# Two-layer transformer block on one core: modulation vectors turned into columns through memory, in portions of 512 columns

## The chip, the cores and the metric

The kernel runs on one core of a Trainium2 chip. The metric is the device time of one execution in microseconds (us); the time of before is the median of three runs. A profile is one execution recorded by the hardware profiler. The engines are PE (TensorE, matmuls) with its weight loads (PEld), DVE (VectorE), ACT (ScalarE), POOL (GpSimd) and SP (SyncE, which issues most of the DMAs). A letter q behind an engine's name means its queue of issued instructions.

## The reference

Two layers, each with a mixer (a gated recurrence, neighbourhood attention and sliding-window attention side by side) and a mixture of 16 experts, over 256 tokens `x` and 256 context tokens `ctx`, all in fp32. Each layer's mixing and normalisation is modulated by six vectors of 1024 numbers, once for `x` and once for `ctx`; these are what the change touches:

```python
D_MODEL = 1024; SEQ = 256; CTX_LEN = 256; DEPTH = 2
def ada_mod(cond, w, b):
    m = (jax.nn.silu(cond) @ w + b)[..., None, :]
    return jnp.split(m, 6, axis=-1)
...
for l in range(DEPTH):
    sh1, sc1, g1, sh2, sc2, g2 = ada_mod(c, w_ada[l], b_ada[l])
    csh1, csc1, cg1, csh2, csc2, cg2 = ada_mod(c_ctx, w_ada[l], b_ada[l])
    h = x * (1.0 + sc1) + sh1;  hc = ctx * (1.0 + csc1) + csh1
    y, yc = mixer(h, hc, ...)
    x = layer_norm(alpha * x + g1 * y, ...);  h2 = x * (1.0 + sc2) + sh2
    f = moe(h2, ...);  x = layer_norm(alpha * x + g2 * f, ...)
    # the same for ctx, except in the last layer
```

`w_ada` has 1024 x 6144 fp32 numbers in each layer, 24 MB, of which each is read once.

## The kernel before

The kernel keeps tokens as columns (feature on the partition), so a modulation vector is wanted as columns: `mod[l]` is a tile of 128 partitions x 6 vectors x 8 blocks x 2 (one for `x`, one for `ctx`). The first two vectors of layer 0 are made at the start, in four short calls of `ada` with their own tiles (`xtp`), and are not touched by the change but for the name of the array that they are loaded from. The other ten vectors of the two layers are made under way, in 20 *portions*: a portion is half a vector, 512 of its 1024 columns, with 2 MB of weights. Portions 0 to 13 run in layer 0's mixer (eight for the other four vectors of layer 0, six for the first three of layer 1), portions 14 to 19 in layer 1's.

A portion is one call of `fill()`, which pops the next from a list and calls `ada`. The calls are woven by hand between projections (`proj`, line 432), attention heads and the recurrence (`weave`, with the counts `FILLS`), and a scheduler then orders each engine's instructions with the program's order as priority. Nothing in the mixer waits for a portion soon: `vectors(0)`, called after portion 7, forms the vectors that layer 0's end uses, sends them to memory (`vd<-md`, line 687, issued by ACT), from which SP loads them back as broadcast rows (line 690).

In a portion, `ada` does this. Two loads of 1 MB go through POOL's queue (line 404) into the two slots of a ring; each waits until PE has read what the slot held, which is the portion before. Then 16 matmuls, each with two columns of the condition (padded to 32) as the stationary operand and 256 columns of weights moving, in four column groups of the array: block `kb` goes to group `kb % 4`, so that four partial sums stand at partitions 0, 32, 64 and 96 of a PSUM bank. Eight use the first slot, eight the second. The trace shows two records for each fp32 matmul, so 32 a portion. ACT copies the bank to SBUF (`vt`, line 414), PE transposes the four 128 x 128 pieces (`adaT`, line 417, a PSUM bank of its own), DVE adds the four partial sums (line 419) and the bias (line 424, two instructions).

The tile `vt` has two buffers and is also used by other copies of ACT. POOL has little else to do in the mixers: the additions of line 1023 in the recurrence, which wait for DVE, and a few fills with a constant.

Of the kernel before, what the change touches and what calls it, by code (L numbers as in the profile page):

```python
# [16 lines left out]
OP = mybir.AluOpType  # L17
AX = mybir.AxisListType

P = 128  # L20
D = 1024
KB = 8
NX = 256
NT = 512
DEPTH = 2
# [38 lines left out]
PIECE = 8 * K  # L64
# [69 lines left out]
def _layout(inp):  # L134
    g = {k: np.asarray(v) for k, v in inp.items()}
    o = {}
# [3 lines left out]
    w = g["w_ada"].reshape(DEPTH, P, KB, 6, P, 4, 2)  # L140
    o["w_ada"] = w.transpose(0, 3, 5, 1, 2, 6, 4).reshape(DEPTH, 24, P, PIECE)
    o["b_ada"] = g["b_ada"].reshape(DEPTH, 6, P, KB).transpose(2, 0, 1, 3).reshape(P, DEPTH * 6 * KB)
# [5 lines left out]
    w = g["w_out"][:, rows, :].reshape(DEPTH, 4, 2, P, D)  # L148
# [42 lines left out]
class _Builder:  # L191
# [117 lines left out]
    def setup(self):  # L309
# [8 lines left out]
        def aload(q):  # L318
            for s in (1, 0):
                self.aw[s, q] = self.g(slots.pop(0), PIECE)  # L320
                nc.sync.dma_start(self.aw[s, q], ap["w_ada"][0, 4 * s + q])

# [72 lines left out]

    def ada(self, l, parts, w=None):
        nc = self.nc
        names = ("xtp", "xtp") if w else ("ada", "adaT")
        if w is None:
            w = []  # L400
            for s, q in parts:
                t = self.g(self.aring[self.na % len(self.aring)], PIECE)
                self.na += 1
                self.late(nc.gpsimd.dma_start(t, self.ap["w_ada"][l, 4 * s + q]))  # L404
                w.append(t)
        pb = self.bank(names[0])
        n = 256 * len(parts)
# [6 lines left out]
        nc.scalar.copy(ev, pb[:, :n])  # L414
        pt = self.bank(names[1])
        for k in range(n // P):
# [107 lines left out]
    def fill(self, n=1):  # L524
        for _ in range(n):
            if self.adas:
                a = self.adas.pop(0)
                self.ada(*a)
                if a[1][-1] == (5, 3):
                    self.vectors(a[0])  # L530

    def mixer(self, l):
# [20 lines left out]
        if l == 0:  # L553
            chunk = lambda l, s: [(l, ((s, q), (s, q + 1))) for q in (0, 2)]
            todo = sum([chunk(0, s) for s in (2, 4, 3, 5)] + [chunk(1, s) for s in (1, 0, 2, 4, 3, 5)], [])
            self.todo = [todo[:8 + EARLY], todo[8 + EARLY:]]
# [70 lines left out]
        self.ering = self.E  # L627
        self.fill(len(self.adas) - n[3])
        if not last:
            self.xres(0)  # L630
# [1551 lines left out]
```

## Time and profile before

| | |
|---|---|
| runs of before | 1181.65, 1181.06, 1179.41 us |
| median | 1181.06 us |
| the profiled execution | 1181.6 us |
| its span in the trace | 1179.7 us |
| mean granted clock of PE | 0.951 |
| layer 0: start, mixer, experts | 0 to 62, 62 to 345, 345 to 680 us |
| layer 1: start, mixer, experts | 680 to 740, 740 to 890, 890 to 1180 us |

The stages are cut by eye at round times. The span runs from the first to the last record of the trace; the execution's own time is 1.9 us longer. The chain is the work that ended last, followed back from the last instruction to what released each step.

### The profile page before, as it was taken

How to read it: one execution, taken by the hardware profiler on the slowest of the kernel's cores; microseconds unless marked ns; L12 is line 12 of the kernel's file. 1: busy time of each engine (PE TensorE's matmuls, PEld its weight loads, DVE VectorE, ACT ScalarE, POOL GpSimd, SP SyncE). 2: the span in 40 equal slices, each digit the busy share in tenths (PEclk: the TensorE clock that was granted, in tenths of full speed). 3: DMA queues.
4: the chain of work that ended last, by engine and by line, in shares of the span. 5: the costliest groups of instructions: out<-in, count | busy, mean ns of one | idle time of the engine just before them, and what ended most of it. 6: DMA issues, size and time to landing. Idle time of an engine off the chain costs nothing.

```text
span 1179.7 us, 18296 instructions
## 1 busy us (share of the span) xinstructions
PE 1069.7 (91%) x6813; PEld 692.8 (59%) x6813; DVE 742.9 (63%) x1703; ACT 533.2 (45%) x875; POOL 129.0 (11%) x137
## 2 busy tenths in 40 slices
PE   5999999999995999999999778999999599999992
PEld 3766776665684777677543378667657344444430
DVE  3456788767689999788623685678786923212125
ACT  2363433446543678588633544543555412211122
POOL 0000011100001134344310000110100000000000
PEclk9999999999995999999999989999999599999995
DMA  9756666644375899799999931744549299999991
GB/s 374 272 214 256 246 249 228 239 160 143 108 285 196 298 362 359 277 351 394 371 406 417 406 111 72 253 155 163 180 153 355 83 410 422 422 421 422 422 384 40
DMA packets 55042, 326.87 MB, mean 277 GB/s; under 512 B 9435, under 2 KB 9691, under 8 KB 19616
## 3 DMA queue, kind: packets, MB, share of 16 engines
q1 hardware_dynamic: 43920, 275.34, 60.5%
q0 software_dynamic: 9152, 50.10, 11.4%
q8 instruction: 56, 0.92, 0.3%
q10 hardware_dynamic: 1872, 0.16, 0.1%
q14 instruction: 42, 0.34, 0.1%
HBM read 316.27 MB, written 13.09 MB: 279 GB/s over the span
## 4 chain that ended last, share of the span: by engine, by line
PE 73%; DVE 14%; ACT 4%; DMA 4%; issue 3%; POOL 1%; SPq 0%; DVEq 0%; ACTq 0%; POOLq 0%
PE proj L432 12%; PE gu L185 9%; PE gu L1647 7%; PE dn L185 4%; PE op L727 4%; PE dn L1647 4%; PE gu L1638 4%; PE first L432 3%; PE ada L411 2%; DMA G<-in_w_ada_dram 2%; PE pt L1140 2%; PE dn L1638 2%; PE hgt L185 2%; PE S L1117 2%; PE py L1147 1%
## 5 line engine op out<-in xcount | busy, mean ns | idle before, releaser
L294 ACT CAST S<-G 128x1024 fp32r<-128x1024 f32 (+2 forms) x83 | 79.3, 958 | 82.0 <-PE proj L432 52.8
L294 ACT CAST T<-G 128x1024 fp32r<-128x1024 f32 (+2 forms) x79 | 78.1, 994 | 84.4 <-PE proj L432 56.1
L304 DVE TENSOR_TENSOR S<-G,S 128x1024 fp32r<-128x1024 f32 (+2 forms) x75 | 85.8, 1147 | 43.7 <-ACT S L294 41.8
L185 PE MATMUL gu<-G,C 128*64 128x512 f32 (+2 forms) x464 | 109.0, 618 | 0.7 <-ACT C L1620 0.7
L304 DVE TENSOR_TENSOR T<-G,T 128x1024 fp32r<-128x1024 f32 (+2 forms) x69 | 82.4, 1198 | 40.5 <-ACT T L294 40.1
L432 PE MATMUL proj<-A,T 128*128 128x512 f32 (+1 forms) x336 | 97.3, 363 | 1.5 <-ACT T L294 1.0
L432 PE MATMUL proj<-A,S 128*128 128x256 f32 (+1 forms) x336 | 89.9, 347 | 1.3 <-DVE S L304 0.9
L1957 DVE SCALAR_TENSOR_TENSOR S<-dn,slot,S 128x512 fp32r<-128x512 f32 x17 | 12.8, 751 | 113.1 <-ACT S L1956 113.0
L432 PEld LDWEIGHTS proj<-A,T 128*128 128x128 f32 x336 | 59.7, 189 | 16.7 <-issue 4.6
L185 PEld LDWEIGHTS gu<-G,C 128*64 128x64 f32 (+2 forms) x464 | 32.7, 135 | 57.7 <-issue 54.0
L432 PEld LDWEIGHTS proj<-A,S 128*128 128x128 f32 x336 | 59.6, 194 | 11.5 <-issue 3.1
L1956 ACT ACTIVATE S<-dn,slot 128x512 fp32r<-128x512 f32 x17 | 11.7, 687 | 89.5 <-PE dn L185 89.5
L1647 PE MATMUL gu<-C,A 128*128 128x512 f32 (+3 forms) x180 | 48.9, 403 | 2.1 <-DVE C L304 2.1
L1647 PE MATMUL gu<-T,A 128*128 128x512 f32 (+3 forms) x174 | 47.6, 404 | 3.3 <-POOL T L302 2.2
L404 POOL DMA_DIRECT2D G<-in_w_ada_dram x40 | 22.1, 552 | 258.6 <-PE ada L411 179.3
L185 PE MATMUL dn<-G,A 128*64 128x512 f32 (+2 forms) x224 | 48.9, 635 | 0.4 <-ACT A L1620 0.4
L1590 POOL DMA_INDIRECT G<-h2d,idx x16 | 22.4, 1397 | 219.7 <-DVE oh L1574 140.7
L294 ACT CAST C<-G 128x1024 fp32r<-128x1024 f32 x38 | 39.8, 1047 | 12.5 <-PE gu L1647 7.2
L1129 ACT ACTIVATE G<-G,nm 128x512 f32<-128x512 f32 x48 | 34.4, 719 | 21.2 <-DVE nm L1127 10.8
L1638 PE MATMUL gu<-G,C 128*64 128x512 f32 x192 | 43.0, 595 | 0.0
L989 DVE TENSOR_TENSOR G<-G 128x256 f32<-128x256 f32 x112 | 42.6, 418 | 0.5
L411 PE MATMUL ada<-G,sT 128*32 128x256 f32 x640 | 40.3, 383 | 1.6 <-DMA G<-in_w_ada_dram 1.6
(483 smaller groups left out, 2392.9 us busy)
## 6 DMA issues: line engine op xcount, KB each, us to landing
G<-in_w_gate_dram SPq DMA_DIRECT2D x62, 1024.0 KB, 8.6
G<-in_w_up_dram SPq DMA_DIRECT2D x60, 1024.0 KB, 9.4
G<-in_w_down_dram SPq DMA_DIRECT2D x60, 1024.0 KB, 12.1
G<-in_w_ada_dram POOLq DMA_DIRECT2D x40, 1024.0 KB, 6.7
G<-in_w_in_dram SPq DMA_DIRECT2D x22, 1024.0 KB, 7.5
G<-in_w_out_dram SPq DMA_DIRECT2D x12, 1024.0 KB, 6.3
G<-in_w_ada_dram SPq DMA_DIRECT2D x8, 1024.0 KB, 16.2
G<-vd SPq DMA_DIRECT2D x12, 512.0 KB, 4.5
```

The costliest lines, as they stand in the source:

```text
L185: return self._then(self.b.nc.tensor.matmul(*a, **k))
L294: self.lasts = [self.nc.scalar.copy(hi, raw)]
L304: self.lasts.append(sub(lo, raw, v))
L411: nc.tensor.matmul(pb[g:g + 32, i * 256:(i + 1) * 256], self.sT[:, kb, :], w[i][:, kb * 256:(kb + 1) * 256], start=kb < 4, stop=kb >= 4, t ...
L432: self.nc.tensor.matmul(pb[:, t], a[:, c], m, start=first and n == 0 and i == 0, stop=last and n == len(kbs) - 1 and i == 2)
L727: nc.tensor.matmul(pbs[tb][h], a, w[j][h], start=n == 0 and i == 0, stop=n == KB - 1 and i == 2)
L989: mul = lambda o, v: tt(o, o, v.to_broadcast([P, n, c]), op=OP.mult)
L1117: nc.tensor.matmul(pb, qT[r, qb * P:(qb + 1) * P], kT[r, :], start=True, stop=True)
L1129: nc.scalar.activation(Pt, Pt, AF.Exp, scale=-1.0, bias=m, accum_out=ls[:, i:i + 1])
L1140: nc.tensor.transpose(pt[:, k * P:(k + 1) * P], Ps[i][:, k * P:(k + 1) * P], self.ident)
L1638: self.pe.matmul(pb[t], h[0][:, g + i], w[o // PIECE][:, o % PIECE:o % PIECE + 512], start=g == 0, stop=g + m == nk, tile_position=(0, i * ...
L1647: nc.tensor.matmul(pbs[j][:cap], h[a][:, k], ws[b][:, c], start=k == 0 and q == 0, stop=k == nk - 1 and q == 2)
```

## The change

`ada` stays as it was for the four calls at the start. A portion is now done in three steps. `send` loads, multiplies and writes; `back` reads; `total` adds. The weights are laid out otherwise on the host, so that a slot holds four blocks `kb` of all 512 columns: a portion is 8 matmuls of 512 columns, the first four from the first slot and the last four from the second. After ACT's copy there are no transposes: POOL issues four DMAs, each of two partitions x 512 numbers (the two rows of a partial sum, 4 KB), to a tile of 8 x 512 in memory. `back` is one DMA on SP's queue that reads the 8 rows so that each of the 128 partitions gets four consecutive numbers of each row: 1024 runs of 16 bytes. `total` adds the four partial sums and the bias with two DVE instructions. `fill` issues the read of a portion one portion later, and its sum two or three later; at the end of a layer's list all sums are made, and `drain` does what is left at the end of layer 1's mixer. So `vectors(0)` comes at the call of portion 10 and no longer at that of portion 7.

```diff
--- before.py
+++ after.py
@@ -138,7 +138,9 @@
     o["xT"] = o["xc"].reshape(NT, P, KB).transpose(1, 2, 0).reshape(P, KB * NT)
     o["cc"] = np.stack([g["c"][0], g["c_ctx"]], axis=-1).reshape(P, KB * 2)
     w = g["w_ada"].reshape(DEPTH, P, KB, 6, P, 4, 2)
-    o["w_ada"] = w.transpose(0, 3, 5, 1, 2, 6, 4).reshape(DEPTH, 24, P, PIECE)
+    o["w_ada0"] = w[0, :, :, :2].transpose(2, 4, 0, 1, 5, 3).reshape(8, P, PIECE)
+    w = g["w_ada"].reshape(DEPTH, P, 2, 4, 6, P, 2, 4)
+    o["w_ada"] = w.transpose(0, 4, 6, 2, 1, 3, 5, 7).reshape(DEPTH, 24, P, PIECE)
     o["b_ada"] = g["b_ada"].reshape(DEPTH, 6, P, KB).transpose(2, 0, 1, 3).reshape(P, DEPTH * 6 * KB)
     w = np.stack([g["w_in"][l][:, _columns(l)] for l in range(DEPTH)]).reshape(DEPTH, P, KB, 11, 2, P)
     o["w_in"] = w.transpose(0, 3, 1, 4, 2, 5).reshape(DEPTH, 11, P, PIECE)
@@ -318,7 +320,7 @@
         def aload(q):
             for s in (1, 0):
                 self.aw[s, q] = self.g(slots.pop(0), PIECE)
-                nc.sync.dma_start(self.aw[s, q], ap["w_ada"][0, 4 * s + q])
+                nc.sync.dma_start(self.aw[s, q], ap["w_ada0"][4 * s + q])
 
         self.first = []
         for q in range(4):
@@ -393,17 +395,45 @@
         nc.vector.tensor_scalar_max(self.lb, self.lb, LB_MIN)
         nc.vector.tensor_scalar(self.lb1m, self.lb, -1.0, 1.0, op0=OP.mult, op1=OP.add)
 
-    def ada(self, l, parts, w=None):
+    def send(self, l, s, h):
         nc = self.nc
-        names = ("xtp", "xtp") if w else ("ada", "adaT")
-        if w is None:
-            w = []
-            for s, q in parts:
-                t = self.g(self.aring[self.na % len(self.aring)], PIECE)
-                self.na += 1
-                self.late(nc.gpsimd.dma_start(t, self.ap["w_ada"][l, 4 * s + q]))
-                w.append(t)
-        pb = self.bank(names[0])
+        w = []
+        for j in range(2):
+            t = self.g(self.aring[self.na % len(self.aring)], PIECE)
+            self.na += 1
+            self.late(nc.gpsimd.dma_start(t, self.ap["w_ada"][l, 4 * s + 2 * h + j]))
+            w.append(t)
+        pb = self.bank("ada")
+        for kb in range(KB):
+            g = 32 * (kb % 4)
+            nc.tensor.matmul(pb[g:g + 32], self.sT[:, kb, :], w[kb // 4][:, kb % 4 * 512:(kb % 4 + 1) * 512],
+                             start=kb < 4, stop=kb >= 4, tile_position=(0, g))
+        ev = self.st("vt", 512)
+        nc.scalar.copy(ev, pb)
+        r = self.dram([8, 512], f"ada{l}{s}{h}")
+        for g in range(4):
+            nc.gpsimd.dma_start(r[2 * g:2 * g + 2, :], ev[32 * g:32 * g + 2])
+        self.sent.append((l, s, h, r))
+
+    def back(self):
+        l, s, h, r = self.sent.pop(0)
+        a = self.st("adab", 32)
+        self.nc.sync.dma_start(a.rearrange("p (r n) -> p r n", n=4), r[:, :].rearrange("r (p n) -> p r n", n=4))
+        self.backs.append((l, s, h, a))
+
+    def total(self):
+        l, s, h, a = self.backs.pop(0)
+        red = self.st("adar", 8).rearrange("p (n s) -> p n s", s=2)
+        self.nc.vector.tensor_reduce(red, a.rearrange("p (g s n) -> p n s g", g=4, s=2), axis=AX.X, op=OP.add)
+        o = (l * 6 + s) * KB + 4 * h
+        b = self.s["b_ada"][:, o:o + 4]
+        self.nc.vector.tensor_tensor(self.mod[l][:, s, 4 * h:4 * h + 4], red, b[:, :, None].to_broadcast([P, 4, 2]), op=OP.add)
+        if (s, h) == (5, 1):
+            self.vectors(l)
+
+    def ada(self, l, parts, w):
+        nc = self.nc
+        pb = self.bank("xtp")
         n = 256 * len(parts)
         for i in range(len(parts)):
             for kb in range(KB):
@@ -412,7 +442,7 @@
                                  start=kb < 4, stop=kb >= 4, tile_position=(0, g))
         ev = self.st("vt", 512)[:, :n]
         nc.scalar.copy(ev, pb[:, :n])
-        pt = self.bank(names[1])
+        pt = self.bank("xtp")
         for k in range(n // P):
             nc.tensor.transpose(pt[:, k * P:(k + 1) * P], ev[:, k * P:(k + 1) * P], self.ident)
         red = self.st("adar", 8).rearrange("p (i k s) -> p i k s", s=2, k=2)[:, :len(parts)]
@@ -524,10 +554,17 @@
     def fill(self, n=1):
         for _ in range(n):
             if self.adas:
-                a = self.adas.pop(0)
-                self.ada(*a)
-                if a[1][-1] == (5, 3):
-                    self.vectors(a[0])
+                self.send(*self.adas.pop(0))
+                while len(self.backs) > 1 - (not self.adas):
+                    self.total()
+                if len(self.sent) > 1:
+                    self.back()
+
+    def drain(self):
+        while self.sent:
+            self.back()
+        while self.backs:
+            self.total()
 
     def mixer(self, l):
         self.tokens_in()
@@ -551,7 +588,8 @@
         self.have = set()
         self.npp = self.npt = 0
         if l == 0:
-            chunk = lambda l, s: [(l, ((s, q), (s, q + 1))) for q in (0, 2)]
+            chunk = lambda l, s: [(l, s, h) for h in range(2)]
+            self.sent, self.backs = [], []
             todo = sum([chunk(0, s) for s in (2, 4, 3, 5)] + [chunk(1, s) for s in (1, 0, 2, 4, 3, 5)], [])
             self.todo = [todo[:8 + EARLY], todo[8 + EARLY:]]
         self.adas = self.todo[l]
@@ -626,6 +664,8 @@
         vecs = self.vecs(l)
         self.ering = self.E
         self.fill(len(self.adas) - n[3])
+        if last:
+            self.drain()
         if not last:
             self.xres(0)
         next(vecs)
```

The order of instructions on the engines moves as follows. In the rows, `in_w_ada_dram` names a load of weights, `ada_581`, `ada_659`, `ada_730`, `ada_804`, `ada_1012`, `ada_1130`, `ada_1237`, `ada_1363`, `ada_1430`, `ada_1538`, `ada_1623`, `ada_1748` are the tiles in memory of portions 0 to 11, and lines of after stand 2 to 40 higher than the same lines of before.

POOL's queue around portion 6 in layer 0's mixer, before (the additions of line 1023 are the recurrence's; the two loads of portion 6 are those on either side of the second addition):

```order
L404 DMA G<-in_w_ada_dram 128x2048 x11
L1023 ISA
L1023 TENSOR_TENSOR G<-G,Sd 128x512
L404 DMA G<-in_w_ada_dram 128x2048
L1023 TENSOR_TENSOR G<-G,Sd 128x512
L404 DMA G<-in_w_ada_dram 128x2048
```

The same place after (the additions are now line 1063):

```order
L404 DMA G<-in_w_ada_dram 128x2048 x2
L415 DMA ada_1012<-vt 2x512 x4
L1063 ISA
L1063 TENSOR_TENSOR G<-G,Sd 128x512
L415 DMA ada_1130<-vt 2x512 x2
L1063 TENSOR_TENSOR G<-G,Sd 128x512
L415 DMA ada_1130<-vt 2x512 x2
L404 DMA G<-in_w_ada_dram 128x2048 x4
L415 DMA ada_1237<-vt 2x512 x4
```

The writes of portions 4 and 5 now stand ahead of the loads of portion 6, two of them and both loads behind the second addition; the four loads in one row are those of portions 6 and 7.

POOL's queue around portion 11, before (the row of six loads ends with both loads of portion 11):

```order
L404 DMA G<-in_w_ada_dram 128x2048 x4
L981 MEMSET G 128x1024
L404 DMA G<-in_w_ada_dram 128x2048 x6
L1023 TENSOR_TENSOR G<-G,Sd 128x512 x2
L404 DMA G<-in_w_ada_dram 128x2048 x4
```

The same place after:

```order
L415 DMA ada_1538<-vt 2x512 x4
L404 DMA G<-in_w_ada_dram 128x2048
L415 DMA ada_1623<-vt 2x512 x4
L1063 TENSOR_TENSOR G<-G,Sd 128x512
L404 DMA G<-in_w_ada_dram 128x2048
L1063 TENSOR_TENSOR G<-G,Sd 128x512
L404 DMA G<-in_w_ada_dram 128x2048 x2
L415 DMA ada_1748<-vt 2x512 x4
```

The single load ahead of `ada_1623` is the first of portion 11; its second now stands behind the four writes of portion 10 and the first addition.

PE's queue around portion 11, before (`lev` belongs to the recurrence, `adaT` are the transposes of portion 11):

```order
L432 MATMUL proj<-C,S 128x512
L432 MATMUL proj<-A,S 128x512
L411 MATMUL ada<-G,sT 32x256 x16
L432 MATMUL proj<-A,T 128x512
L432 MATMUL proj<-B,T 128x512
L432 MATMUL proj<-A,T 128x512 x2
L417 MATMUL adaT<-con,vt 128x128 x4
L999 MATMUL lev<-G 128x128 x8
```

The same place after:

```order
L462 MATMUL proj<-A,S 128x512
L409 MATMUL ada<-G,sT 32x512 x4
L1039 MATMUL lev<-G 128x128 x8
L462 MATMUL proj<-A,T 128x512
L462 MATMUL proj<-B,T 128x512
L462 MATMUL proj<-A,T 128x512 x2
L409 MATMUL ada<-G,sT 32x512 x4
L462 MATMUL proj<-B,T 128x512
```

The transposes are gone, the portion is eight matmuls instead of sixteen, and its second half stands behind the `lev` group and three rows of a projection.

SP's queue in layer 0's mixer, before (`Yd<-Sd` clears a tile in memory, `in_w_in_dram` are weights of projections):

```order
L266 DMA G<-in_w_in_dram 128x2048 x2
L695 DMA G<-in_xc_dram 128x1024
L266 DMA G<-in_w_in_dram 128x2048 x3
L614 DMA Yd_947<-Sd 128x512 x16
L266 DMA G<-in_w_in_dram 128x2048 x3
L690 DMA G<-vd_1465 128x1024 x2
L266 DMA G<-in_w_out_dram 128x2048 x2
```

The same place after:

```order
L268 DMA G<-in_w_in_dram 128x2048 x2
L421 DMA adab<-ada_581 128x8x4
L421 DMA adab<-ada_659 128x8x4
L421 DMA adab<-ada_730 128x8x4
L268 DMA G<-in_w_in_dram 128x2048
L652 DMA Yd_908<-Sd 128x512 x16
L421 DMA adab<-ada_804 128x8x4
L268 DMA G<-in_w_in_dram 128x2048
L421 DMA adab<-ada_1012 128x8x4
L268 DMA G<-in_w_in_dram 128x2048
L421 DMA adab<-ada_1130 128x8x4
L268 DMA G<-in_w_in_dram 128x2048
```

A read `adab<-ada` stands ahead of each load of projection weights from the fifth on, three of them ahead of that fifth.

## Rows read from the trace of the kernel before

**Rows 1.** The page: busy us, share of the span and instructions by engine.

```profile
PE 1069.7 (91%) x6813; PEld 692.8 (59%) x6813; DVE 742.9 (63%) x1703; ACT 533.2 (45%) x875; POOL 129.0 (11%) x137
```

**Rows 2.** Windows: stretch, length, busy us (instructions) by engine, clock, DMA share, GB/s.

```profile
62.00:130.00 68.00, 66.70 (x427) 46.64 (x426) 43.88 (x113) 32.31 (x55) 4.26 (x8) 1.00 0.69 257
```

**Rows 3.** Groups of the tile adaT.

```profile
L417 PE MATMUL adaT<-con,vt x80: 270/273/329, 77.2 to 830.2; 128*128 128x128 f32 x80
```

**Rows 4.** Pieces of the chain: start us, us, what; the transposes and what hangs on them.

```profile
77.36 0.50 PE adaT L417 x4
...
100.46 0.10 DVE adar L419
100.99 0.15 DVE mod L424 x2
...
212.47 0.48 ACT vt L414
...
214.66 1.09 PE lev L999 x16
215.75 3.19 PE proj L432 x13
...
830.01 0.44 PE adaT L417 x4
```

**Rows 5.** Pieces of the chain: whole portions, and a later group of the same width.

```profile
826.54 1.86 PE ada L411 x32
...
981.74 1.85 PE gu L185 x16
```

**Rows 6.** Groups of line 185 on PE by form.

```profile
L185 PE MATMUL gu<-T,C x24: 592/592/617, 969.5 to 1133.0; 128*32 128x512 f32 x16, 128*64 128x512 f32 x8
```

**Rows 7.** Pieces of the chain: portions in halves, and one that other work cuts.

```profile
95.76 1.07 PE ada L411 x16
...
229.09 0.55 PE ada L411 x2
...
230.23 1.86 PE ada L411 x30
```

**Rows 8.** Groups of the tile ada: ACT's copy.

```profile
L414 ACT COPY vt<-ada x20: 565/588/621, 76.5 to 829.1; 128x512 f32<-128x512 f32 x20
```

**Rows 9.** Groups of line 404 and their landing.

```profile
L404 POOL DMA_DIRECT2D G<-in_w_ada_dram x40: 530/530/750, 48.2 to 794.4; - x40
...
DMA to landing us min/median/max: 5.1/6.7/11.0
```

**Rows 10.** Timeline of POOL: start us, us, what, idle before and what ended it.

```profile
146.58 0.56 POOL L404 DMA_DIRECT2D G<-in_w_ada_dram  x1 [4.75 <-PE ada L411]
149.01 1.27 POOL L1023 TENSOR_TENSOR G<-G,Sd 128x512 f32<-128x512 f32 x1 [1.87 <-DVE Sd L1003]
150.22 0.55 POOL L404 DMA_DIRECT2D G<-in_w_ada_dram  x1
...
210.09 0.53 POOL L404 DMA_DIRECT2D G<-in_w_ada_dram  x1 [0.33 <-PE ada L411]
217.29 1.28 POOL L1023 TENSOR_TENSOR G<-G,Sd 128x512 f32<-128x512 f32 x1 [6.66 <-DVE Sd L1003]
```

**Rows 11.** Timeline of PE at the portions that those loads feed.

```profile
156.04 1.07 PE L411 MATMUL ada<-G,sT 128*32 128x256 f32 x16
158.06 1.07 PE L411 MATMUL ada<-G,sT 128*32 128x256 f32 x16 [0.96 <-DMA G<-in_w_ada_dram]
...
218.87 1.93 PE L411 MATMUL ada<-G,sT 128*32 128x256 f32 x32
```

**Rows 12.** Pieces of the chain that are loads.

```profile
107.80 10.89 DMA G<-in_w_in_dram
...
150.22 7.80 DMA G<-in_w_ada_dram
```

**Rows 13.** Line 687, vd<-md, three DMAs: us from issue to landing.

```profile
DMA to landing us min/median/max: 5.0/5.0/5.1
```

## The prediction

> **What bounds the kernel now.** I read the page first, for which engine is full: PE is busy 91% of the span, DVE 63%, ACT 45%, POOL 11% [rows 1]. Next the windows of the mixers, where the portions run: from 62 to 130 us PE is busy 66.70 of 68 us at the full granted clock, DVE 43.88, POOL 4.26 [rows 2]; the other stretches with portions read alike. So PE is the bound where the change works, and there is room on DVE and POOL. Then the chain, for which of a portion's steps lie on it. Its matmuls do, and so do its transposes: pieces like the 0.50 us at 77.36 and the 0.44 us at 830.01 stand there 17 times, for 16 of the 20 portions, 6.91 us together; in two places DVE's sum of a portion is on it too (0.10 and 0.15 us), and once PE waits for ACT's copy, 0.48 us at 212.47 [rows 4]. Last the loads: each starts when PE has left its slot and lands after 5.1 to 11.0 us, 6.7 at the middle [rows 9], and one of them, 7.80 us from 150.22, is on the chain [rows 12].
>
> **What it takes away.** The transposes: 80 matmuls of 273 ns each [rows 3], which pipeline to 0.44 us for four [rows 4]. Twenty portions of these would be 8.8 us of PE; I count the 6.91 us that lie on the chain, since where the chain runs elsewhere PE has a wait to give back. With them go the wait for ACT's copy, 0.5 us, and the two pairs of DVE steps, 0.5 us, because the sums are now made portions later. That is 7.9 us.
>
> **Half as many matmuls.** A portion's 32 records of 256 columns take 1.86 us on the chain, 58 ns each. A later group of 16 records of 512 columns, with the same 32 stationary columns, takes 1.85 us [rows 5, 6]. So the time goes with the columns, and the same columns in half the matmuls gain nothing. The bounds are 0 and, if each matmul had a price of its own, 0.93 us a portion, 18.6 us in all; I take 0, since the row of the same form says so. [...]
>
> **Portions cut by other work.** In the new order of PE the portions 1, 2, 13 and 16 have other matmuls between the four that run side by side in the column groups. Portion 12 was cut so before: its first matmul took 0.55 us alone and the other 30 records still 1.86 us [rows 7]. Four such cuts are 2.0 us (bounds: 1.6 at a quarter of 1.86 each, and 2.2). Portions 3, 9, 11 and 18 are newly done in two separate halves; a half costs 1.07 us instead of 0.93 [rows 7], so 0.14 a half, at most 0.28 for each portion; I take 0.2, 0.8 us in all.
>
> **POOL's queue.** Each write is one more DMA that POOL issues: 530 ns by the loads' row [rows 9], 0.55 back to back [rows 10]. Four of them, behind ACT's copy of 0.59 us [rows 8], hold the queue until 2.8 us after PE has finished the portion. A second load of the next portion that stands behind them starts that much later, where before it followed PE's last read by some 0.33 us [rows 10]. By the order this happens to portions 3, 6, 9, 11, 13, 16 and 18; portion 13 has time to spare. The scheduler sets the second halves of most of these later too. The two where POOL also does an addition cost most:
> Portion 6: both loads stand behind the second addition, which ended at 149.01 + 1.27 = 150.28, and two writes, 1.1 us. The first load then starts at 151.4 instead of 146.58 and lands at 156.5 to 158.1 (5.1 to 6.7 us), where PE came for it at 156.04: a wait of 0.5 to 2.1, say 1.3. PE's present wait of 0.96 at 158.06 [rows 11] then falls away, since the second half stands later: 0.3 net.
> Portion 11: the copy of portion 10 ended at 212.47 + 0.48 = 212.95 [rows 4]; four writes to 215.15; the addition of 1.28 to 216.4, if DVE has it ready by then (it ran at 217.29, but its matmuls now stand ahead of a projection); so the load starts at 216.4 instead of 210.09 [rows 10] and lands at 221.5 to 223.1. PE comes to the first half at 218.87 [rows 11]; 0.93 for it, 1.09 for the recurrence's group and four projection matmuls of 3.19/13 = 0.25 us each [rows 4] put the second half at 221.9: a wait of 0 to 1.2, say 0.4.
> For portions 3, 9, 16 and 18 the bounds are 0 and 2.8 us each; I take 1.0 us for the four, near the lower end, because the second half was moved back too. The losses on this queue are 1.7 us.
>
> **Edits at no cost, and their cover.** The read comes a portion after the write and the sum one or two after that, so some ten to twenty microseconds lie between. The nearest row is the transfer to memory in small runs, `vd<-md`, with 5.0 us to landing [rows 13]; the upper bound for a small DMA here is the 11.0 us of the loads [rows 9]. Without the cover a portion would wait write plus read, 10 to 22 us, but DVE's sum would be late and not PE, because no one asks for the vectors before the mixer's end. `vectors(0)` comes three portions later, and the loads of its rows stand ahead of the first load of `w_out` on SP; neither is wanted before the output projection. DVE saves about 0.1 us a portion, off the chain.
>
> **The sum.** 1181.6 (the profiled execution) - 7.9 + 2.0 + 0.8 + 1.7 = 1178.2 us. That execution stood 0.5 us above the median of the runs, so 1177.7 us, 0.3% faster than 1181.06. By this kernel's runs about 0.2%, 2.4 us, is what a measurement can tell from no change.
>
> **The rivals.**
> *POOL's queue gives it all back.* Nothing in the order keeps a late second load from being waited for. If six portions wait the whole 2.8 us, that is 16.8 instead of 1.7: 1192.8 us; at half of it, 8.4, 1184.4. It decides from 5.1 us on, 0.85 us a portion. For it speaks that one such load is on the chain already [rows 12]; against it, that PE has other work between the halves.
> *The transposes were not what PE waited on.* Where the 6.91 us are taken out, the chain passes to the next thing that is late: a load of weights, DVE's recurrence, ACT's casts. Two places of the chain show how: the load of 10.89 us at 107.80 and that of 7.80 at 150.22 [rows 12] do not get shorter when PE is early. If half of the 7.9 us is lost so, the sum is 1181.6 - 4.0 + 4.5 = 1182.1, less 0.5: 1181.6 us, no change. Here I also put SP's queue: the read of portion 2 stands ahead of the projection load at 107.80. That portion's matmuls end at 95.76 + 1.07 = 96.83; copy and writes, 2.8, to 99.6; landing 5.1 to 11.0 later, at 104.7 to 110.6. So the load is late by nothing or up to 2.8 + 0.3 us.
> *The matmuls have a price each.* 18.6 us more: 1159.1 us. For it speaks that 32 records in 1.86 us are also evenly spaced, 58 ns each; against it the 16 records in 1.85 us [rows 5].
>
> **How the numbers follow.** My forecast has a chance of 0.5, POOL's queue giving back 5 us or more 0.22, a chain that passes elsewhere 0.23, a price for each matmul 0.05. Of the forecast's own spread (1174 to 1180) the part above 1178.7, about a sixth of its chance, lies within 0.2% of before. So faster 0.42 + 0.05 = 0.47, same 0.08 + 0.23 = 0.31, slower 0.22. The range leaves out the cheap matmuls and the worst of POOL's queue: 1170 (transposes worth 8.8 us and the cuts, halves and waits almost free, with some gain from the larger matmuls) to 1187 (POOL's queue at two thirds of its bound).
>
> **What the changed profile would show.** No `adaT`, and PE busy some 5 us less in the mixers, with a portion still 1.85 us (right) or near 0.95 (the third rival). In the list of who waited for the loads of line 404, PE stays under 4 us or rises to 10 and more (the first rival). The reads on SP wait long ahead of the load of projection weights at about 107, and the layer 0 experts start as early as the mixer ends. The prediction is wrong if the mixers end at the same time as before although the transposes are gone.

## The result, and the profile after

The changed kernel takes 1190.27 us, median of 7 runs (1186.63 to 1194.83), against 1179.87 of the kernel before in the same comparison. The ratio is 1.0084, interval 1.0059 to 1.0109: slower by 10 us, and outside the forecast's range of 1170 to 1187. The profiled execution took 1193.23 us, with a span of 1191.4.

The page of the kernel after, its row of busy time:

```profile
PE 1072.4 (90%) x6413; PEld 680.0 (57%) x6413; DVE 740.9 (62%) x1683; ACT 534.0 (45%) x875; POOL 171.8 (14%) x217
```

PE lost 400 instructions against [rows 1] (80 transposes, 320 matmuls) and yet is busy 2.7 us longer, so some of its work ran slower. The windows of the kernel after show where (columns as in [rows 2], the clock third from the end):

```profile
62.00:130.00 68.00, 64.56 (x333) 41.50 (x331) 36.30 (x87) 32.99 (x56) 12.33 (x24) 0.97 0.67 236
200.00:280.00 80.00, 71.81 (x438) 45.92 (x436) 54.91 (x138) 31.14 (x60) 18.51 (x31) 0.91 0.66 219
215.00:220.00 5.00, 1.86 (x13) 0.47 (x11) 3.43 (x8) 4.94 (x8) 0.56 (x1) 1.00 1.02 401
220.00:225.00 5.00, 3.10 (x14) 1.37 (x16) 0.13 (x1) 0.96 (x4) 0.17 (x1) 0.50 0.64 218
225.00:230.00 5.00, 5.00 (x24) 4.10 (x25) 3.22 (x8) 0.00 (x0) 3.38 (x6) 0.50 0.14 7
230.00:235.00 5.00, 5.00 (x30) 3.98 (x32) 5.00 (x15) 1.23 (x3) 1.71 (x2) 0.98 0.62 210
850.00:855.00 5.00, 3.31 (x18) 1.56 (x15) 4.20 (x12) 3.45 (x7) 0.00 (x0) 0.99 0.78 215
855.00:860.00 5.00, 4.04 (x16) 2.68 (x14) 3.23 (x12) 2.09 (x6) 1.87 (x3) 0.50 0.58 210
860.00:865.00 5.00, 5.00 (x14) 2.33 (x12) 4.33 (x14) 1.88 (x4) 1.13 (x2) 0.50 0.02 3
```

From 215 to 220 us PE is busy 1.86 of 5 us; from 220 to 230 the granted clock is 0.50, although PE is full again from 225 on. From 850 to 865 the same happens: 3.31 of 5 us busy, then 0.50. In the kernel before, the windows of these two places read 1.00 throughout. What made PE idle stands in the timeline of PE after, around its portions 9 (205.12 and 210.20, two halves) and 10 (215.79 and 221.90); columns as in [rows 10]:

```profile
205.12 1.06 PE L409 MATMUL ada<-G,sT 128*32 128x512 f32 x8
206.12 1.16 PE L1039 MATMUL lev<-G 64*128 64x128 f32 x16
...
210.20 1.07 PE L409 MATMUL ada<-G,sT 128*32 128x512 f32 x8
...
215.79 1.06 PE L409 MATMUL ada<-G,sT 128*32 128x512 f32 x8
221.90 1.94 PE L409 MATMUL ada<-G,sT 128*32 128x512 f32 x8 [5.04 <-DMA G<-in_w_ada_dram]
...
224.76 2.08 PE L1039 MATMUL lev<-G 64*128 64x128 f32 x16
```

PE waits 5.04 us for the second load of portion 10. The same half of a portion then takes 1.94 us and not 1.06, the same 16 matmuls of the recurrence 2.08 and not 1.16. The timeline of POOL after says why the load came late:

```profile
199.29 0.56 POOL L404 DMA_DIRECT2D G<-in_w_ada_dram  x1 [11.63 <-PE ada L409]
200.76 1.99 POOL L415 DMA_DIRECT2D ada<-vt  x4 [0.91 <-ACT vt L412]
202.73 0.55 POOL L404 DMA_DIRECT2D G<-in_w_ada_dram  x1
206.52 0.54 POOL L404 DMA_DIRECT2D G<-in_w_ada_dram  x1 [3.24 <-PE ada L409]
211.59 0.53 POOL L404 DMA_DIRECT2D G<-in_w_ada_dram  x1 [4.53 <-PE ada L409]
```

Portion 9's second load (202.73) stands behind portion 8's four writes, 3.4 us behind its first (199.29). PE doesn't wait for it, since the order puts portion 9's second half 5 us behind the first. But so its slot comes free 5 us later, and portion 10's loads are issued 5.07 us apart (206.52 and 211.59). Before, portion 9 was one piece, and the loads behind it were issued 0.86 us apart:

```profile
198.30 0.53 POOL L404 DMA_DIRECT2D G<-in_w_ada_dram  x1 [10.12 <-PE ada L411]
199.16 0.53 POOL L404 DMA_DIRECT2D G<-in_w_ada_dram  x1 [0.33 <-PE ada L411]
```

The chain of the kernel after has this load and three reads on it (start us, us, what):

```profile
74.29 1.85 PE ada L409 x16
...
86.55 10.85 DMA adab<-ada
97.42 0.21 DVE adar L427
...
179.79 11.14 DMA adab<-ada
190.95 0.22 DVE adar L427
...
211.59 10.26 DMA G<-in_w_ada_dram
221.90 1.94 PE ada L409 x8
...
843.34 4.94 DMA ada<-vt
848.43 2.27 DMA adab<-ada
850.73 0.22 DVE adar L427
851.28 1.23 DVE S L306
```

A portion in one piece takes 1.85 us, as forecast. A read, its sum on DVE, and behind the sum DVE's other work. At 97.42 that is the recurrence, a split of weights (line 306) and the attention's steps, and PE waits for the last of them:

```profile
107.05 1.69 PE L1180 MATMUL pt<-con,G 128*128 128x128 f32 x8 [3.13 <-DVE G L1177]
```

Behind the last sum stand the split at 851.28 and the attention's line 1162, for which PE waits 1.32 us at 853.23. The last portion's write and read at 843 to 851 have nothing to cover them. The waits of the kernel after from 62 to 900 us (us in total, times, longest), the group of the writes, and the landing of the reads:

```profile
DVE adar L427 <- DMA adab<-ada: 11.7, 5, 6.1
...
PE ada L409 <- DMA G<-in_w_ada_dram: 5.6, 3, 5.0
```

```profile
L415 POOL DMA_DIRECT2D ada<-vt x80: 499/505/802, 78.9 to 843.3; - x80
```

```profile
DMA to landing us min/median/max: 2.1/2.6/11.1
```

A read lands after 2.6 us at the middle and 11.1 at most. In the kernel before, DVE's sums waited 11.7 us as well, for the transposes:

```profile
DVE adar L419 <- PE adaT L417: 11.7, 6, 6.0
```

So the total of this wait is no measure of its harm. What stands behind the sum at that moment matters, as the wait at 107.05 shows.

**Where the time is lost.** Below, for stretches of some 10 us of the kernel before, the median over DVE's instructions there (those that occur equally often in both kernels) of how much later they start; minus is earlier. One execution each, against before's profiled one of 1181.6 us:

```
stretch of before that begins at   130   200   240   300   820   860  1160 us
changed kernel                     5.7   7.9  16.1  16.6  11.8  17.1  13.5
changed kernel, a second time     -1.2  -0.5   7.8   9.2   5.3  10.7  15.9
loads first (below)                4.0   2.9  14.8  15.5  11.5  17.0  12.8
late sums (below)                 -0.7  -0.9   2.6   1.6   0.7   4.8   1.3
loads first and late sums         -0.5  -2.7  -1.0   0.6  -3.6  -4.9  -3.1
no trip (below)                   -0.9  -6.0  -3.6  -4.6  -6.7  -8.6 -10.3
before, no transposes             -1.3  -5.4  -5.2  -4.8  -9.5  -5.3  -8.6
```

Two losses stand in both executions of the changed kernel: 8 us between 200 and 240, where PE waits for portion 10's load, and 5 us between 820 and 860, where the last sum stands. The second can't be put down to the trip alone: the kernel before without its transposes, which has no trip, loses 4 us there too, with a granted clock of 0.81 and 0.68 from 830 to 850. The 5.7 us by 130 stand only in the first (the wait of 6.1 us before the sum at 97.42), and what lies behind 900 differs by several microseconds between executions of one kernel.

### The profile page after: what moved, and what is told of

It reads as the page before. It is cut to its first block, busy times and chain, and to the rows that moved or that the text cites. A ratio compares the mean times of both kernels' runs of the same rounds, so it can differ in the third digit from the quotient of the medians.

```text
span 1191.4 us, 17683 instructions
## 1 busy us (share of the span) xinstructions
PE 1072.4 (90%) x6413; PEld 680.0 (57%) x6413; DVE 740.9 (62%) x1683; ACT 534.0 (45%) x875; POOL 171.8 (14%) x217
## 3 DMA queue, kind: packets, MB, share of 16 engines
q0 software_dynamic: 11712, 50.44, 11.7%
## 4 chain that ended last, share of the span: by engine, by line
PE 66%; DVE 17%; DMA 7%; ACT 4%; issue 3%; POOL 1%; SPq 1%; ACTq 0%; DVEq 0%; POOLq 0%
PE proj L462 9%; PE gu L187 9%; PE gu L1687 7%; PE dn L187 4%; PE op L767 4%; PE dn L1687 4%; PE gu L1678 4%; PE first L462 3%; DMA G<-in_w_ada_dram 3%; DMA adab<-ada 2%; PE pt L1180 2%; PE dn L1678 2%; PE ada L409 2%; PE hgt L187 2%; PE S L1157 1%
## 5 line engine op out<-in xcount | busy, mean ns | idle before, releaser
L187 PE MATMUL gu<-G,C 128*64 128x512 f32 (+2 forms) x464 | 105.8, 596 | 0.7 <-ACT C L1660 0.7
L415 POOL DMA_DIRECT2D ada<-vt x80 | 40.7, 516 | 95.2 <-ACT vt L412 94.5
L409 PE MATMUL ada<-G,sT 128*32 128x512 f32 x320 | 47.0, 620 | 5.6 <-DMA G<-in_w_ada_dram 5.6
L1996 ACT ACTIVATE S<-dn,slot 128x512 fp32r<-128x512 f32 x17 | 11.7, 687 | 87.8 <-PE dn L187 87.8
L2106 POOL TENSOR_TENSOR G<-G 128x512 f32<-128x512 f32 x2 | 2.5, 1266 | 318.8 <-DVE sm L2098 317.9
```

Of the source, the lines that this page charges most:

```text
L187: return self._then(self.b.nc.tensor.matmul(*a, **k))
L409: nc.tensor.matmul(pb[g:g + 32], self.sT[:, kb, :], w[kb // 4][:, kb % 4 * 512:(kb % 4 + 1) * 512], start=kb < 4, stop=kb >= 4, tile_posit ...
L415: nc.gpsimd.dma_start(r[2 * g:2 * g + 2, :], ev[32 * g:32 * g + 2])
```

## The experiments

My first theory was that the trip through memory costs more than the transposes, through what waits behind its pieces: (a) the sums stand in DVE's queue ahead of the mixer's other work; (b) the writes on POOL move the loads; (c) the reads on SP hold back the projection loads. The rivals were that the transposes were worth nothing, and that the wider matmuls or the new order cost time. In each block below, the ratio is to the kernel before on the same chip.

**e1_notrans: the kernel before without its transposes.**

```diff
-        pt = self.bank(names[1])
-        for k in range(n // P):
-            nc.tensor.transpose(pt[:, k * P:(k + 1) * P], ev[:, k * P:(k + 1) * P], self.ident)
+        pt = ev
...
```

> The kernel before with the transposes left out: DVE sums from ACT's copy instead, so the modulation vectors do not hold the right numbers. If the transposes' 6.9 us on the chain, with the waits around them, are worth what the prediction says (7.9 us), this runs about 8 us faster than before, 1172. If the chain passes elsewhere, within 2 us of before.

1172.80 us, ratio 0.9940 (0.9918 to 0.9961): 7.0 us. Within this interval the transposes were worth what the chain said.

**e2_wide: the kernel before with portions in 16 matmuls of 512 columns, transposes kept.**

```diff
...
+            for kb in range(KB):
+                g = 32 * (kb % 4)
+                nc.tensor.matmul(pb[g:g + 32], self.sT[:, kb, :], w[kb // 4][:, kb % 4 * 512:(kb % 4 + 1) * 512],
+                                 start=kb < 4, stop=kb >= 4, tile_position=(0, g))
...
```

> The kernel before with only the eight matmuls of 512 columns; transposes kept, no trip through memory. If the time goes with the columns: within 2 us of before, a portion 1.85 us. If each matmul has a price of its own: up to 18 us faster, a portion near 0.95 us. If cutting a portion in halves or its new weight layout is what costs: several us slower.

1180.28 us, ratio 1.0004 (0.9988 to 1.0020). The group of this kernel's portions:

```profile
L413 PE MATMUL ada<-G,sT x320: 592/592/617, 73.6 to 826.4; 128*32 128x512 f32 x160
```

One matmul takes 592 ns, as the row of the same form did [rows 6], and half as many of them save nothing.

**e3_actwrite: the changed kernel with ACT issuing the writes.**

```diff
-            nc.gpsimd.dma_start(r[2 * g:2 * g + 2, :], ev[32 * g:32 * g + 2])
+            nc.scalar.dma_start(r[2 * g:2 * g + 2, :], ev[32 * g:32 * g + 2])
```

> The changed kernel with the four writes of a portion issued by ACT, behind its own copy, instead of by POOL, so that no load of weights stands behind a write. Theory POOL (late second loads): the 5.6 us that PE waits for weights fall below 2, and the time falls by 4 to 6 us, to about 1185. Theory sums (DVE waits for reads that land late, with the recurrence queued behind): DVE still waits some 11 us for the reads and the time stays within 3 us of the changed kernel.

1180.62 us, ratio 1.0006 (0.9988 to 1.0025): nearly all of the loss is gone. The group of the writes, portion 9 in the timeline of PE, and the waits in this kernel:

```profile
L415 ACTq DMA_DIRECT2D ada<-vt x80: 229/265/544, 77.3 to 826.6; - x80
```

```profile
193.41 1.92 PE L409 MATMUL ada<-G,sT 128*32 128x512 f32 x16
```

```profile
DVE adar L427 <- DMA adab<-ada: 12.6, 5, 5.7
```

With POOL's queue free the order changes: portion 9 is in one piece at 193.41, its successor's loads are 0.86 us apart as before, and PE waits 3.4 us for loads in all, at most 1.5 for one. DVE waits as long for the reads as in the changed kernel. So (b) costs, by way of the order; that the order moved because POOL's issues count in it is argued from these rows, not tried apart.

**e4_latesum: the changed kernel with each sum two portions later and behind DVE's latest split of a projection; five tiles for the reads instead of two.**

```diff
...
-        self.nc.vector.tensor_reduce(red, a.rearrange("p (g s n) -> p n s g", g=4, s=2), axis=AX.X, op=OP.add)
+        add = self.nc.vector.tensor_reduce(red, a.rearrange("p (g s n) -> p n s g", g=4, s=2), axis=AX.X, op=OP.add)
+        self.behind(add, self.lasts[1])
...
-                while len(self.backs) > 1 - (not self.adas):
+                while len(self.backs) > (3 if self.adas else 0):
```

> The changed kernel with each sum two portions later and held behind DVE's latest split of projection weights, five buffers for the reads; POOL's and SP's queues as in the change. Theory sums: DVE's 11.7 us of waiting for reads in the mixers nearly vanish, but for the last portion, and the time falls by 6 to 9 us, to 1181 to 1184. Theory POOL: within 2 us of the changed kernel.

1181.03 us, ratio 1.0016 (0.9996 to 1.0036): this too gives back 8 us, with the writes still on POOL. DVE waits 1.9 us for a read, once. The timeline of PE shows portion 10 again in two halves, the second still waiting, but less:

```profile
206.86 1.06 PE L409 MATMUL ada<-G,sT 128*32 128x512 f32 x8
210.63 1.51 PE L409 MATMUL ada<-G,sT 128*32 128x512 f32 x8 [2.29 <-DMA G<-in_w_ada_dram]
```

The 8 us are thus not the sums' alone. The halves of portions 9 and 10 stand as in the changed kernel, but the load is waited for 2.29 us and not 5.04, having landed 7.3 us after its issue and not 10.26; between 200 and 240 this kernel loses 3.5 us and not 8. What the sums cost by themselves is left to e14 and e15.

**e5_both: e3 and e4 together.** Both edits above.

> Writes by ACT and late sums together. The two edits alone took 9 to 10 us each from the changed kernel. If they mend two separate losses: about 1171, what leaving the transposes out gave. If they mend one and the same stall between 200 and 260 us (one wait of PE, and the half clock behind it), the sum is not twice as large: 1177 to 1181, and what stays is the end of layer 1's mixer, where PE idles and the clock drops to half for some 10 us.

Ratio 1.0006 (0.9980 to 1.0032): no better than either alone. The two do not add.

**e6_early and e7_all: the last portion of layer 1 one fill earlier, alone, and with e3 and e4.**

```diff
-FILLS = ((4, 5, 4, 1), (3, 2, 1, 0))
+FILLS = ((4, 5, 4, 1), (3, 3, 0, 0))
```

> The changed kernel, but the last portion of layer 1 is started one stage earlier, so that its trip through memory is over when its sum stands ahead of the split of output weights on DVE. Theory of the uncovered last trip: the wait and the half clock between 850 and 870 us go, the time falls by 5 to 7 us, to 1183 to 1185. If that stop is due to something else (the recurrence, the output weights): within 2 us of the changed kernel.

> Writes by ACT, late sums, the last portion a stage earlier. If the three are the whole loss, the transposes' gain comes out: 1172 to 1175, faster than before by 0.4 to 0.6%. If another loss hides behind them: 1178 or more.

e6: ratio 1.0103 (1.0063 to 1.0143); e7: 0.9986 (0.9957 to 1.0014). In e6 the stop at 850 is gone, but DVE now waits 5.0 us for the last sum at about 821. The loss had moved. Whether the edit is worth anything stays open: against the same kernel without it, it gave +2 (e6), -2 (e7) and, below, +5 us (e16).

**e8_actread: the changed kernel with ACT issuing the reads.**

```diff
-        self.nc.sync.dma_start(a.rearrange("p (r n) -> p r n", n=4), r[:, :].rearrange("r (p n) -> p r n", n=4))
+        self.nc.scalar.dma_start(a.rearrange("p (r n) -> p r n", n=4), r[:, :].rearrange("r (p n) -> p r n", n=4))
```

> The changed kernel with the reads issued by ACT instead of by SP, sums and writes where the change has them. If the reads land late because they stand on SP behind loads that wait for their slot: DVE's wait for them falls from 11.7 to under 5 us and the time to 1182 to 1185. If it is the place of the sums, too soon behind any read: no change, 1188 to 1192.

1195.28 us, ratio 1.0133 (1.0090 to 1.0176), and DVE waits 17.6 us. The landing of the reads:

```profile
DMA to landing us min/median/max: 2.2/2.2/6.3
```

Issued by ACT, no read lands later than 6.3 us, where on SP one took 11.1. Yet the sums wait longer in all (8.1 us for portion 3's and 5.4 for the last), and the time does not fall although SP's loads now stand behind no read. So (c) is not borne out.

**e9_noread and e10_nowrite: e4 without the reads, and without reads and writes** (the sums add the table of biases in their place).

```diff
-        a = self.st("adab", 32)
-        self.nc.sync.dma_start(a.rearrange("p (r n) -> p r n", n=4), r[:, :].rearrange("r (p n) -> p r n", n=4))
+        a = self.s["b_ada"][:, 0:32]
```

```diff
-        for g in range(4):
-            nc.gpsimd.dma_start(r[2 * g:2 * g + 2, :], ev[32 * g:32 * g + 2])
```

> The changed kernel without the reads; the sums add the bias table in place of the read tile (so the modulation vectors are not the right numbers), at the places of the late sums. POOL still issues the writes. If the reads' own traffic or their place on SP costs time beyond the sums' waiting: faster than the late sums (1181.0) by more than 3 us. If what is left is POOL's queue and the separated halves: 1179 to 1183.

> As the run without reads, and without the writes as well: a portion is loads, eight matmuls and ACT's copy. If writes on POOL are what is left: down to what leaving out the transposes gave, 1171 to 1174. If the wide portions, the new order or the late vectors themselves cost: 1178 or more.

e9: 1178.92 us, ratio 0.9985 (0.9961 to 1.0009), 3.7 us below e4 by the ratios with intervals that overlap, so that a cost of the reads beyond the sums' waiting is not told from none. e10: 1171.28 us, ratio 0.9929 (0.9905 to 0.9954). Everything in the change but the trip makes the kernel 8.4 us faster; the trip costs 18 us, and of them some 6.6 are the writes (e9 against e10). The window of e10 that answers to the bad one after:

```profile
200.00:280.00 80.00, 74.84 (x452) 45.05 (x452) 59.44 (x154) 39.16 (x78) 7.12 (x8) 1.00 0.59 213
```

Full clock, and 3 us more of PE's work done in 80.

**e11_poolread: e7 with the reads issued by POOL.**

```diff
-        self.nc.sync.dma_start(a.rearrange("p (r n) -> p r n", n=4), r[:, :].rearrange("r (p n) -> p r n", n=4))
+        self.nc.gpsimd.dma_start(a.rearrange("p (r n) -> p r n", n=4), r[:, :].rearrange("r (p n) -> p r n", n=4))
```

> Writes by ACT, late sums, last portion a stage earlier, as in the run with all three, and the reads issued by POOL, so that SP's loads of projection and output weights stand behind no read. If reads on SP hold those loads up: 1173 to 1176. If reads ahead of the loads of weights on POOL delay them instead: 1180 or more.

Ratio 0.9988 (0.9971 to 1.0004), as e7. Once the sums are late and ACT writes, it makes no difference whether SP or POOL issues the reads.

**e12_again: the changed kernel unchanged**, for a second profile (no edit).

> The changed kernel once more, for a second profile: which of its stalls are the same in two executions. Theory POOL expects PE's wait of 5 us for the second load of portion 10 again, with the clock at half behind it; theory sums expects DVE's wait for reads of 11 to 12 us again; the uncovered last trip expects the half clock at the end of layer 1's mixer again. Median 1188 to 1192.

1190.16 us, ratio 1.0087 (1.0053 to 1.0120). The second row of the shift table; its waits and windows:

```profile
PE ada L409 <- DMA G<-in_w_ada_dram: 6.3, 3, 5.4
...
DVE adar L427 <- DMA adab<-ada: 5.5, 5, 2.4
```

```profile
210.00:215.00 5.00, 1.14 (x8) 0.20 (x8) 0.13 (x1) 1.97 (x6) 0.00 (x0) 0.56 0.88 334
215.00:220.00 5.00, 5.00 (x27) 3.79 (x24) 1.39 (x4) 0.58 (x1) 1.98 (x4) 0.50 0.17 21
```

The 5 us wait of PE and the half clock behind it come back; the wait of 6.1 us at 97 does not (0.3 us here).

**e13_act_noread: e7 without the reads.** The edit of e9 on e7.

> Writes by ACT, late sums, last portion a stage earlier, and no reads (the sums add the bias table, so the modulation vectors are not the right numbers). Beside the run with all three (1178.5) and the run with neither writes nor reads (1171.3). If the writes cost wherever they are issued (ACT's time, the copy's buffer held until they land): 1176 to 1179. If on this route it is the reads: 1171 to 1173.

1177.23 us, ratio 0.9965 (0.9939 to 0.9990). Some 4 us of the writes may remain when ACT issues them (against e10, with intervals that overlap; e6's edit is in it too).

**e14_loadfirst and e15_loadfirst_late: the loads of the next portion ahead of a portion's writes on POOL, alone and with e4's late sums.**

```diff
...
         r = self.dram([8, 512], f"ada{l}{s}{h}")
+        if self.adas:
+            self.ahead.append(self.fetch(*self.adas[0]))
         for g in range(4):
-            nc.gpsimd.dma_start(r[2 * g:2 * g + 2, :], ev[32 * g:32 * g + 2])
+            wr = nc.gpsimd.dma_start(r[2 * g:2 * g + 2, :], ev[32 * g:32 * g + 2])
+            if self.ahead:
+                self.behind(wr, self.ahead[0][1])
...
```

> The changed kernel with the two loads of the next portion put ahead of the writes of a portion on POOL's queue, sums and reads where the change has them. Theory POOL: PE's wait of 5 us and the half clock behind it go, the time falls by 5 us or more, to 1185 or less. If the sums alone are the loss: within 3 us of 1190.

> Next loads ahead of the writes on POOL, and late sums. Beside the late sums alone (1181.0). If what the writes still cost there (7.6 us) is the delay of second loads: 1173 to 1176, faster than before. If it is their issue on POOL ahead of the recurrence's additions, the later order of the portions on PE or the copy's buffer: 1179 or more.

e14: 1193.28 us, ratio 1.0099 (1.0063 to 1.0136). e15: 1176.29 us, ratio 0.9974 (0.9943 to 1.0005). From e14, the row of DVE's waits from 62 to 900 us, then its longest wait for a read behind 200 us with DVE's step behind the sum and PE's wait for that step; from e15, the row of waits:

```profile
DVE adar L436 <- DMA adab<-ada: 33.4, 9, 8.2
```

```profile
240.90 0.20 DVE L436 TENSOR_REDUCE adar<-adab 128x8 f32<-128x32 f32 x1 [6.38 <-DMA adab<-ada]
...
241.23 0.42 DVE L1012 TENSOR_TENSOR tmp<-rot,con 128x256 f32<-128x256 f32 x1
...
241.70 1.11 PE L1189 MATMUL pt<-con,G 128*128 128x128 f32 x4 [4.14 <-DVE tmp L1012]
```

```profile
DVE adar L437 <- DMA oh<-ada: 4.3, 2, 2.6
```

This is the pair that decides. In e14 PE waits at most 1.6 us for a load, so POOL's part is mended, and the kernel is no faster than the changed one: the writes stand behind the next loads in POOL's queue, and DVE's sums wait 33.4 us for the reads instead of 11.7. The rows show what that does: DVE idles 6.38 us before a sum, the step behind it (line 1012) is late, and PE waits 4.14 us for that step; behind the wait seven matmuls of a portion took 3.64 us (242.74), where seven of portion 1 took 1.92 in the changed kernel. Make the same sums late, and 15 us come back by the ratios (13 against e17, the same kernel again), while PE's waits for loads are about the same (2.9 us in all in e14, 2.4 in e15). With both mended the kernel stands at the kernel before.

**e16_loadfirst_all and e17_loadfirst_late2: e15 with e6's edit, and e15 once more.** No new edit.

> Next loads ahead of the writes, late sums, and the last portion a stage earlier. If the uncovered last trip is a loss of its own (half clock at the end of layer 1's mixer): 2 to 5 us faster than without the third edit, 1171 to 1174, and faster than before by 0.5% or more. If not: 1175 to 1178.

> Next loads ahead of the writes and late sums once more, for a narrower interval and a second profile: 1174 to 1178, 0.2 to 0.5% faster than before.

e16: ratio 1.0028 (1.0005 to 1.0051); DVE waits 5.0 us for the last sum at 801, and the window behind it falls to a clock of 0.64. e17: 0.9991 (0.9972 to 1.0010). No version with the whole trip is clearly faster than the kernel before; e15, e7 and e11 have the lowest ratios. Only e13, without the reads, is below 1 with its whole interval.

## Why the prediction was wrong

**Right: the transposes, and half as many matmuls.** Forecast 7.9 us with the two small waits; 7.0 in e1, and 8.4 in e10 with the new portions. The price of a portion follows the columns: 1.85 us in 16 records after, 1.86 in 32 before, and e2's ratio is 1.0004. The rival of a price for each matmul falls, and so does the one by which the chain passes elsewhere: without the trip the gain arrives in full. SP's read ahead of the projection load, named there, is not what costs: with the reads off SP the time does not fall (e8).

**Not seen: cuts and halves, 2.8 us.** e10 has the wide portions without the trip, and is no slower than e1 (0.9929 and 0.9940, with intervals that overlap). Its order differs from the changed kernel's (portion 9 in one piece at 193.25), so the term's worth in time stays unmeasured. Its size on PE can be read from the changed kernel, at portion 1:

```profile
83.77 1.04 PE L409 MATMUL ada<-G,sT 128*32 128x512 f32 x2
...
85.81 1.92 PE L409 MATMUL ada<-G,sT 128*32 128x512 f32 x14
```

The other work begins at 84.75, 0.98 us after the first matmul, and the other seven take what a whole portion takes. So a cut is 1.0 us and not 0.5, and four are 4 us, not 2.0: the forecast took the price from a matmul of 256 columns (the lower bound there should also read 1.9, four quarters of 1.86). Two halves (1.06 and 1.07) cost 0.2 us more than a whole portion (1.92), as forecast. That e10, cut alike at portion 1, is still no slower stays open.

**The step that failed: "Edits at no cost, and their cover".** It said that a late read would leave "DVE's sum ... late and not PE, because no one asks for the vectors before the mixer's end". No one asks for the vectors, but behind the sum in DVE's queue stand its steps of the recurrence and the attention and the splits of weights, and PE asks for those. The kernel after shows it at 97, 190 and 850 us, where DVE idled 6.11, 2.28 and 2.09 us before the sum and started the step behind it within 0.6 us of the sum's start, and e14 at 241 (DVE idle 6.38 us, then PE 4.14). Nor was the cover the whole of "ten to twenty microseconds": the read at 179.79 took 11.14 us from its issue, and the last portion has no portion behind it. The step should have asked what is queued behind the waiting instruction, not who reads its result. What it cost: 13 to 15 us with the loads first (e14 against e17 and e15, by the ratios); with the loads as the change has them up to 8 (changed kernel against e4), of which a part is the shorter wait for the load.

**The second: POOL's queue was sized at 1.7 us.** It priced portions 6 and 11, and gave 3, 9, 16 and 18 one microsecond together, because their second halves had been moved back. At portion 9 that is what happened, without a wait; but the half that was moved back held its slot, and the next portion's load, 10.26 us beside other loads, came 5.04 us late. The term stopped at the portion whose load was behind the writes and did not follow its slot to the next. Behind the wait the granted clock was 0.50: half a portion and 16 matmuls of the recurrence together took 4.02 us instead of 2.22. Wait and clock together are about the 8 us that the shift table has between 200 and 240. The forecast counted a wait at its own length only.

**The sum, by the runs.** As ratios of 1180 us: everything but the trip -8.4 (e10); the trip with loads first and late sums 6.4 more (mean of e15 and e17, -2.0); loads as the change has them 3.9 more (e4, +1.9); the sums at the change's place 8 more (+9.9). That makes the 10 us. The intervals are 2 to 4 us to either side, so the 3.9 is hardly told from nothing. The order of the steps matters: putting the loads first and no more shows nothing (e14), though taking the writes off POOL shows nearly all (e3).

**Near, for another reason: the first rival.** POOL's queue at half of its bound was 1184.4 us, at the whole 1192.8. The time lies between, but POOL alone does not make it: with its loads put first the time stays (e14). The sign that was named for this rival did not decide: PE's wait for the loads is 5.6 us, neither under 4 nor 10 and more.

**Open.** What the last 6.4 us of the trip are: `vt` held until the writes are done, the issuing engine's time, or traffic. A copy buffer of its own for the writes was not tried. And why e3, whose DVE waits 12.6 us for reads, loses little by them: behind its longest wait, 5.75 us at 206.81, PE waits only 1.23 us for DVE (209.11). Its sums may wait where little stands behind them, but no run takes that apart. And how much of the 5 us between 820 and 860 is the trip's.

## What to carry to other kernels

When a result goes through memory, price the instruction that waits for it by what stands behind it in its engine's queue, even if no one needs the result (in e14 DVE idled 6.38 us before a sum, and PE waited 4.14 for the step behind it); put it as late as its buffers allow. Small DMAs added to an engine that also issues loads can change the order and hold a slot longer, as they did here (two loads issued 5.07 us apart, 0.86 before); follow the slot, not only the queue. The mendings did not add here (ratios 1.0006 in e3, 1.0016 in e4, 1.0006 with both): test them in pairs, since one alone showed nothing (e14, 1.0099) or nearly everything (e3).

## What the runs showed of the hardware

- Behind a stretch of 5 us in which PE was busy 1.86, its granted clock was 0.50 for about 10 us (220 to 230), though PE was full again from 225; in e12 it was 0.56 and 0.50 from 210 to 220, with PE busy 1.14 and 5.00 of 5 us. The wait of 5.04 us and the clock behind it together cost about 8 us, an estimate from the shift table.
- A read of 32 elements for each partition in runs of 16 B, issued by SP, landed in 2.1 us at best, 2.6 at the middle and 11.1 at worst; issued by ACT (e8), in 2.2, 2.2 and 6.3.
- A write of 4 KB takes POOL 505 ns to issue and ACT 265 (e3); the read takes SP 371.
- Two executions of one kernel that agree in the total (1193.2 and 1195.6 us) differ by 7 us in where the time stands at 130 us.
